# A hybrid convolution and recurrence block: HGRN's readout turned by VectorE and through memory, ahead of the convolution, and a layer norm with summed blocks

## The chip, the cores and the metric

The kernel runs on one core of a Trainium2 chip. The metric is the device time of one execution in microseconds (us), from the program's start to its end; a run lists it, and a profile of one execution gives a span that is a little shorter. A core has five engines that run their own instruction queues in order: TensorE (PE, matrix products, with its weight loads PEld), VectorE (DVE), ScalarE (ACT), GpSimd (POOL) and SyncE (SP). They wait for each other by semaphores. Transfers between memory and the core's on-chip memory are issued on such a queue and move on 16 DMA engines.

## The reference

One layer of a diffusion backbone, on 256 latent tokens of 2048 channels (and 256 context tokens that only prepare the states of the recurrence). All numbers are float32. What the change touches is the token mixer:

```
h = modulate(rms_norm(x, norm_pre_mix), sh_m, sc_m)
p_i, p_ff, p_fb, p_q, p_g, p_cv, p_cg, p_gc, p_gh = split_proj(h @ w_in)
o = hgrn_bidir(...)                    # 256 tokens x 8 heads x 128
# hgrn_readout
o = rms_norm(o, norm_g)                # mean of squares over the 128 channels of a head
y_h = (o * silu(p_g)) @ hgrn_out_w     # 1024 -> 2048
# conformer_branch
u = axial_dwconv(val * sigmoid(gate))  # 1024 channels: 512 along rows (31 taps), 512 along columns
u = silu(layer_norm(u, ln_g, ln_b))    # mean and variance over the 1024 channels
y_c = u @ conv_pw_w                    # 1024 -> 2048
y = (sigmoid(p_gc) * y_conv + sigmoid(p_gh) * y_hgrn) @ w_out
```

Behind it come a gated residual and a squared-ReLU MLP of 8192 channels.

## The kernel before

**Weights.** Each weight is read from memory as tiles of 128x1024 (`raw`, 512 KB), by transfers that SP issues into a ring of five buffers. For precision each tile is split: ScalarE writes a rounded high part `whi` (L124), and VectorE the remainder `wlo = raw - whi` (L127), into rings of four such pairs. The activations are split alike (`split`, L240), so a product is three products: high by high, high by low, low by high (`mm3r`). In `tokens` the tokens lie on the partitions of the result: one k step of 128 channels is 12 products of 512 columns (L188) for one pair `whi`, `wlo`. A projection of 2048 by 2048 has two groups of 16 k steps; the last three k steps of a group are done bank by bank, so that the evacuation of one bank lies beside the products of the next. Into the stream of weights further tiles are mixed that VectorE alone takes (matrix-vector products of the modulation, L1314 and L1301).

**Background work.** Everything else that has to happen beside the products is written as Python generators in a deque `bg`. After each k step `pump(us)` gives credit; the first three generators of the deque are advanced in turn. A generator that yields a number is charged that many us; one that yields `None` ends its turn for this k step, so some `None`s in a row let as many k steps go by. The instructions are written into the engines' queues at that place, each behind the weights' splits that were written last, and stay in that order. `finish` drains one generator.

**Order around the change.** Projection of the convolution's gates and values; then the generator `conv` is pushed (L829) and silu of HGRN's gate `p_g` is computed (`ev_g`, L831 to L839). Behind it the two readouts are pushed (L840, L841), four heads each, so in the deque they stand behind the convolution. Then come the two merge gates' projections (`ev_gate(0)`, `ev_gate(1)`, L853 and L854), 64 k steps in all, through which the background work is pumped. Then the product with `hgrn_out_w` (`ev_ho`), for which the readouts have to be finished, then the one with `conv_pw_w` (`ev_pw`), for which the convolution has to be finished, and the output projection and the MLP.

**`readout(j)`** (L1551) makes the reciprocal norms of four heads, scales the head's result `o` by it and by silu(g) on VectorE (L1562, two instructions of 128 columns per head, tokens on the partitions), then turns both halves on TensorE (L1567) into a bank, so that channels lie on the partitions; ScalarE takes the bank times the gain into the high part (L1570), VectorE the rest into the low part (L1571). The parts lie in `rp`, the operand of the heads' product.

**`conv`** (L1574) does 31 taps for four blocks of 128 channels on VectorE (L1584, L1586: 128x256 each, four to a charge of 1.6), then four blocks along the columns (L1592, L1595), and then the layer norm over 1024 channels, which lie as eight blocks of 256 columns in the two pages `y`. `sums` reduces each page's four blocks on VectorE (L1603) into one half of `lnred`; `mean` multiplies both halves by a 128x128 matrix that holds 1/1024 (`self.mean`), with two products that add up in one bank (L1609). That is done twice, for the mean and for the squares, and the normed result goes through silu into `cv`, the operand of the convolution's product.

**Turning without TensorE.** The MLP of the kernel before already turns its hidden result another way: VectorE turns blocks of 32x32 (`turn_blocks`, L1250), a page goes out to memory in one transfer and comes back in four that put the blocks in place (`swapped`, L1284 and L1287, issued by GpSimd). `turn_hidden` lets ten `None`s go by before it reads the page that comes back.

Of the kernel before, what the change touches and what calls it, by code (L numbers as in the profile page):

```python
# [8 lines left out]
F32 = mybir.dt.float32  # L9
# [3 lines left out]
AF = mybir.ActivationFunctionType  # L13
ALU = mybir.AluOpType

P = 128
T = 256
# [9 lines left out]
TW = 1024  # L27
# [7 lines left out]
PB = 4  # L35
# [102 lines left out]
class Kernel:  # L138
# [247 lines left out]
    def run(self):  # L386
        nc, a = self.nc, self.a
# [142 lines left out]
        for i in range(2):  # L530
            ps = self.bank()
# [172 lines left out]
        for k in range(KT):  # L704
            ps = self.bank()[:, :T]
            nk = KT if k < WHOLE else KP
            for t in range(nk // 4):
                st.fetch_to(FETCH)
                w = st.whole()
                for j in range(4):  # L710
                    g, n = 32 * j, 4 * t + j
# [68 lines left out]
        heads = []  # L780
        for h in range(NH):
            accs = []
            for d in range(2 * (h > 0)):
                accs.append(self.bank())
                for hf in range(2):
                    hi, lo = st.next()
# [50 lines left out]
            nc.vector.tensor_tensor(s, acc, s, op=ALU.mult)  # L837

        self.tokens(hlat, ev_g, 1.3, groups=1)  # L839
        for j in range(2):  # L840
            heads.append(self.push(self.readout(j)))  # L841


        gp = [[None] * 4, [None] * 4]
# [17 lines left out]

        self.tokens(self.operand(self.rp), ev_ho, 1.3, nk=8)
        self.finish(conv)
        zh, zl = self.pages(4, F32R, "zh"), self.pages(4, F32R, "zl")

# [684 lines left out]
    def readout(self, j):  # L1551

        nc = self.nc
        while self.ended < 4 * (j + 1):
            yield None
        r = self.osq[:, 8 * j:8 * j + 8]
        self.rstd(r, r, 1.0 / P)
        for h in range(4 * j, 4 * j + 4):
            o = self.at(self.on, h)
            for tb in range(2):  # L1560
                s = o[:, tb * P:(tb + 1) * P]
                nc.vector.scalar_tensor_tensor(s, s, self.osq[:, 2 * h + tb:2 * h + tb + 1], self.sg[tb][:, h * P:(h + 1) * P], op0=ALU.mult, op1=ALU.mult)  # L1562
            yield 0.5
            yield None
            ps = self.bank()
            for tb in range(2):
                nc.tensor.transpose(out=ps[:, tb * P:(tb + 1) * P], in_=o[:, tb * P:(tb + 1) * P], identity=self.v["ident"])  # L1567
            g = self.v["hng"][:, h:h + 1]
            hi, lo = self.rp[h][:, :T], self.rp[h][:, T:]
            nc.scalar.activation(out=hi, in_=ps[:, :T], func=AF.Copy, scale=g)  # L1570
            nc.vector.scalar_tensor_tensor(lo, ps[:, :T], g, hi.bitcast(F32), op0=ALU.mult, op1=ALU.subtract)  # L1571
            yield 0.5

    def conv(self, uhv, uvv):  # L1574
        nc, v = self.nc, self.v
        y = self.pages(2, F32, "conv")
        dww = v["dww"].rearrange("p (b w) -> p b w", b=8)
        out = lambda b: self.at(y, b).rearrange("p (r w) -> p r w", r=ROWS)
        n = 0
        for w in (PAD, *(w for w in range(CW) if w != PAD)):  # L1580
            for b in range(4):
                src, c = uhv[b][:, :, w:w + GW], dww[:, b, w:w + 1]
# [7 lines left out]
        for b in range(4, 8):  # L1590
            o, u = out(b), uvv[:, b - 4, :].rearrange("p (r w) -> p r w", r=ROWS)
# [5 lines left out]
        bc = lambda r: r.rearrange("p (o t) -> p o t", o=1).broadcast_to([P, PB, T])  # L1597
        kt_ = lambda pg: pg[:, :TW].rearrange("p (b t) -> p b t", b=PB)

        def sums(src):  # L1600
            red = self.small(512, "lnred")
            for j in range(2):
                nc.vector.tensor_reduce(red[:, j * T:(j + 1) * T], kt_(src[j]).rearrange("p b t -> p t b"), axis=mybir.AxisListType.X, op=ALU.add)  # L1603
            return red

        def mean(red):
            m = self.bank()
            for j in range(2):
                nc.tensor.matmul(m[:, :T], self.mean, red[:, j * T:(j + 1) * T], start=(j == 0), stop=(j == 1))  # L1609
            return m  # L1610
        red = sums(y)
        yield 2.4
        yield None
        yield None
        m = mean(red)
        yield None
        mu = self.small(T, "lnmu")
# [1 line left out]
        for j in range(2):  # L1619
            nc.vector.tensor_tensor(kt_(y[j]), kt_(y[j]), bc(mu), op=ALU.subtract)  # L1620
        yield 2.2
        sq = self.pages(2, F32, "lnsq")
        for j in range(2):
            nc.scalar.activation(out=sq[j][:, :TW], in_=y[j][:, :TW], func=AF.Square)
        yield None
        red = sums(sq)
        yield 2.4
        yield None
        yield None
        m = mean(red)  # L1630
        yield None
        self.rstd(m[:, :T], mu, 1.0)
# [4 lines left out]
        for b in range(0, 8, 2):  # L1637
            o, e = self.at(y, b, 2), self.at(sq, b, 2)
            for j in range(2):
                i, s = b + j, slice(j * T, (j + 1) * T)  # L1640
# [86 lines left out]
```

## Time and profile before

| | us |
|---|---|
| three runs: lowest, median, highest | 1624.18, 1625.0, 1625.57 |
| the profiled execution, its own time | 1623.7 |
| its span | 1621.9 |
| mean granted TensorE clock over the span | 0.999 |

The span is the time from the first to the last instruction that the profile records; 1.8 us of the execution lie around it. A row of the timeline gives a start, a duration, the engine, the line, the operation with its output and inputs, the shape, and in brackets an idle time ahead of it with what ended it; "x4" stands for that many alike in a row. A row of the windows gives a stretch, its length, and the busy time of each engine in it. A row of the groups gives the least, the median and the longest duration in ns, and when the group ran. The rows themselves stand in the prediction, beside what is read from them.

### The profile page before, as it was taken

The page shows a single profiled execution, that of the slowest core. Times are in us where ns is not written, and L with a number is a line of the kernel's source. Part 1 is how long each engine was busy: PE and PEld are TensorE (multiplying, and loading weights), DVE is VectorE, ACT ScalarE, POOL GpSimd, SP SyncE. Part 2 cuts the span into 40 slices and gives each one's busy share as a digit, 9 for nine tenths or more (in the row PEclk, how much of TensorE's full clock was granted, in tenths as well). Part 3 has the DMA queues.
Part 4 walks back from the last instruction along what each step waited for, and adds up shares of the span by engine and source line. Part 5 has one row for each costly group of instructions (what it writes and reads, how often), then busy time and mean ns, then how long its engine had stood idle before and what let it go on. Part 6 is the DMA issues. An engine that isn't in the chain of part 4 may idle for free.

```text
span 1621.9 us, 22046 instructions
## 1 busy us (share of the span) xinstructions
PE 1606.9 (99%) x8195; PEld 1322.7 (82%) x8195; DVE 1154.8 (71%) x1678; ACT 804.7 (50%) x1166; POOL 52.2 (3%) x98
## 2 busy tenths in 40 slices
PE   7999999999999999999999999999999999999998
PEld 5768888888888888888888888888888888888887
DVE  5886887787868889967887765555665665655556
ACT  6553454455654444653446665444443454435543
POOL 0000000000000000000000001000110011001000
PEclk9999999999999999999999999999999999999999
DMA  9997954444666556678887378866887688677773
GB/s 378 409 388 269 326 192 140 156 146 141 221 206 212 189 192 205 231 271 299 324 289 266 135 255 263 271 205 224 288 277 246 213 270 270 228 242 239 232 219 116
DMA packets 109148, 391.00 MB, mean 241 GB/s; under 512 B 12912, under 2 KB 13808, under 8 KB 109040
## 3 DMA queue, kind: packets, MB, share of 16 engines
q1 hardware_dynamic: 102096, 368.34, 66.3%
q0 software_dynamic: 6656, 20.99, 4.4%
q8 instruction: 64, 1.05, 0.3%
q14 instruction: 44, 0.36, 0.1%
q10 hardware_dynamic: 288, 0.26, 0.0%
HBM read 379.06 MB, written 10.49 MB: 240 GB/s over the span
## 4 chain that ended last, share of the span: by engine, by line
PE 92%; DMA 5%; DVE 1%; issue 1%; ACT 1%; SPq 0%; ACTq 0%; DVEq 0%
PE bank L188 80%; PE bank L255 5%; PE bank L257 3%; DMA raw<-wi 2%; DMA rawpage<-wm 1%; PE bank L1495 1%; DMA rawpage<-wms 1%; DMA x<-ctx 1%; PE bank L1541 0%; PE bank L1539 0%; PE bank L1530 0%; DVE wlo L127 0%; DMA raw<-wpw 0%; PE bank L1502 0%; ACT whi L124 0%
## 5 line engine op out<-in xcount | busy, mean ns | idle before, releaser
L127 DVE TENSOR_TENSOR wlo<-raw,whi 128x1024 fp32r<-128x1024 f32 x488 | 593.5, 1223 | 335.1 <-ACT whi L124 329.2
L124 ACT ACTIVATE whi<-raw 128x1024 fp32r<-128x1024 f32 x488 | 512.7, 1059 | 592.0 <-PE bank L188 388.2
L188 PE MATMUL bank<-whi,h 128*128 128x512 f32 x2160 | 674.1, 390 | 2.0 <-DVE h L673 1.1
L188 PEld LDWEIGHTS bank<-whi,h 128*128 128x128 f32 x2160 | 405.2, 188 | 87.4 <-DVE h L673 2.0
L188 PE MATMUL bank<-wlo,h 128*128 128x512 f32 x1080 | 420.9, 390 | 1.1 <-DVE wlo L127 1.1
L188 PEld LDWEIGHTS bank<-wlo,h 128*128 128x128 f32 x1080 | 202.8, 188 | 44.7 <-DVE wlo L127 3.0
L188 PE MATMUL bank<-whi,hidh 128*128 128x512 f32 x503 | 195.0, 388 | 0.0
L188 PE MATMUL bank<-wlo,hidh 128*128 128x512 f32 x503 | 195.0, 388 | 0.0
L188 PE MATMUL bank<-whi,hidl 128*128 128x512 f32 x503 | 195.0, 388 | 0.0
L188 PE MATMUL bank<-h,whi 128*128 128x512 f32 x512 | 164.7, 402 | 0.1
L188 PEld LDWEIGHTS bank<-h,whi 128*128 128x128 f32 x512 | 91.8, 188 | 23.4 <-issue 5.8
L188 PEld LDWEIGHTS bank<-wlo,hidh 128*128 128x128 f32 x503 | 94.5, 188 | 19.5
L188 PEld LDWEIGHTS bank<-whi,hidl 128*128 128x128 f32 x503 | 94.5, 188 | 19.3
L188 PEld LDWEIGHTS bank<-whi,hidh 128*128 128x128 f32 x503 | 94.5, 188 | 19.2
L188 PE MATMUL bank<-h,wlo 128*128 128x512 f32 x256 | 100.2, 391 | 0.0
L255 PE MATMUL bank<-h,whi 128*128 128x512 f32 x384 | 97.2, 395 | 0.0
L255 PEld LDWEIGHTS bank<-h,whi 128*128 128x128 f32 x384 | 69.0, 189 | 12.6
L1314 DVE SCALAR_TENSOR_TENSOR raw<-raw,silu_row 128x1024 f32<-128x1024 f32 x64 | 76.8, 1220 | 1.6 <-DMA raw<-wmt 1.5
L1301 DVE SCALAR_TENSOR_TENSOR gacc<-raw,silu_c,gacc 128x1024 f32<-128x1024 f32 x60 | 76.7, 1279 | 0.3 <-DMA raw<-wm 0.3
L188 PEld LDWEIGHTS bank<-h,wlo 128*128 128x128 f32 x256 | 48.0, 188 | 10.1
L257 PEld LDWEIGHTS bank<-h,wlo 128*128 128x128 f32 x384 | 52.4, 190 | 3.8
L257 PE MATMUL bank<-h,wlo 128*128 128x256 f32 x384 | 53.5, 282 | 0.0
(251 smaller groups left out, 1355.0 us busy)
## 6 DMA issues: line engine op xcount, KB each, us to landing
raw<-w SPq DMA_DIRECT2D x256, 512.0 KB, 4.7
raw<-wi SPq DMA_DIRECT2D x172, 512.0 KB, 4.3
raw<-wmt SPq DMA_DIRECT2D x64, 512.0 KB, 4.1
raw<-wm SPq DMA_DIRECT2D x64, 512.0 KB, 4.7
rawpage<-wm SPq DMA_DIRECT2D x42, 512.0 KB, 10.1
raw<-wo SPq DMA_DIRECT2D x32, 512.0 KB, 4.6
raw<-who SPq DMA_DIRECT2D x16, 512.0 KB, 4.9
raw<-wpw SPq DMA_DIRECT2D x16, 512.0 KB, 5.7
```

Source lines behind the costliest of these rows:

```text
L124: kn.his.append(nc.scalar.activation(out=hi, in_=raw, func=AF.Copy))
L127: kn.los.append(nc.vector.tensor_tensor(lo, raw, hi.bitcast(F32), op=ALU.subtract))
L188: ins = fn(*args, **kw)
L255: nc.tensor.matmul(bank, w[0][:, cut(i)], x(k)[2], start=(k == 0), stop=False)
L257: nc.tensor.matmul(bank[:, T:], w[1][:, cut(i)], x(k)[0], start=False, stop=(k == nk - 1))
L1301: nc.vector.scalar_tensor_tensor(acc, raw, s, acc, op0=ALU.mult, op1=ALU.add)
L1314: nc.vector.scalar_tensor_tensor(raw, raw, 1.0, self.srow, op0=ALU.mult, op1=ALU.mult, accum_out=self.dot[:, 32 * j + b:32 * j + b + 1])
L1495: nc.tensor.matmul(ps[64 * g:64 * g + 64, n * P + b * 64:n * P + b * 64 + 64], left[:, o:o + 64], right[:, r:r + 64] if right is not None ...
```

## The change

Three things. The readouts are put at the head of the deque, so their work is written ahead of the convolution's taps (`appendleft` of 1 and then 0, so readout 0 comes first). A readout scales its four heads, turns them with two block turns into a page `oflip` (L1251), sends this out and back by `swapped` (L1285, L1288), lets eight `None`s go by, and then for each head ScalarE takes the piece of `back` times the gain into `gained` (L1577), which is split into high and low like any activation (L240). And the norm's `sums` adds the eight blocks with three additions, of 1024, 512 and 256 columns, into one `lnred` of 256 columns, so that `mean` is one product. The page for the squares is taken earlier, as it holds the sums in between.

```diff
@@ -837,8 +837,9 @@
         self.tokens(hlat, ev_g, 1.3, groups=1)
-        for j in range(2):
-            heads.append(self.push(self.readout(j)))
+        for j in (1, 0):
+            heads.append(self.readout(j))
+            self.bg.appendleft(heads[-1])
@@ -1560,15 +1561,21 @@
                 nc.vector.scalar_tensor_tensor(s, s, self.osq[:, 2 * h + tb:2 * h + tb + 1], self.sg[tb][:, h * P:(h + 1) * P], op0=ALU.mult, op1=ALU.mult)
-            yield 0.5
+            if h % 2:
+                yield 0.5
+        flip = self.page(F32, "oflip")
+        for n in range(2):
+            self.turn_blocks(flip, n, self.on[j][:, n * 512:(n + 1) * 512])
+            yield 0.7
+        back = self.swapped(flip).rearrange("p (i b r) -> p b i r", i=4, b=8)
+        for _ in range(8):
             yield None
-            ps = self.bank()
-            for tb in range(2):
-                nc.tensor.transpose(out=ps[:, tb * P:(tb + 1) * P], in_=o[:, tb * P:(tb + 1) * P], identity=self.v["ident"])
-            g = self.v["hng"][:, h:h + 1]
-            hi, lo = self.rp[h][:, :T], self.rp[h][:, T:]
-            nc.scalar.activation(out=hi, in_=ps[:, :T], func=AF.Copy, scale=g)
-            nc.vector.scalar_tensor_tensor(lo, ps[:, :T], g, hi.bitcast(F32), op0=ALU.mult, op1=ALU.subtract)
+        for n in range(PB):
+            h = PB * j + n
+            g, src = self.v["hng"][:, h:h + 1], back[:, 2 * n:2 * n + 2]
+            t = self.small(T, "gained")
+            nc.scalar.activation(out=t.rearrange("p (b i r) -> p b i r", b=2, i=4), in_=src, func=AF.Copy, scale=g)
+            self.split(t, self.rp[h][:, :T], self.rp[h][:, T:])
             yield 0.5
@@ -1597,18 +1604,19 @@
-        def sums(src):
-            red = self.small(512, "lnred")
-            for j in range(2):
-                nc.vector.tensor_reduce(red[:, j * T:(j + 1) * T], kt_(src[j]).rearrange("p b t -> p t b"), axis=mybir.AxisListType.X, op=ALU.add)
+        def sums(src, both):
+            nc.vector.tensor_tensor(both[:, :TW], src[0][:, :TW], src[1][:, :TW], op=ALU.add)
+            nc.vector.tensor_tensor(both[:, :512], both[:, :512], both[:, 512:TW], op=ALU.add)
+            red = self.small(T, "lnred")
+            nc.vector.tensor_tensor(red, both[:, :T], both[:, T:512], op=ALU.add)
             return red
         def mean(red):
             m = self.bank()
-            for j in range(2):
-                nc.tensor.matmul(m[:, :T], self.mean, red[:, j * T:(j + 1) * T], start=(j == 0), stop=(j == 1))
+            nc.tensor.matmul(m[:, :T], self.mean, red, start=True, stop=True)
             return m
-        red = sums(y)
+        sq = self.pages(2, F32, "lnsq")
+        red = sums(y, sq[0])
@@ -1619,11 +1627,10 @@
-        sq = self.pages(2, F32, "lnsq")
-        red = sums(sq)
+        red = sums(sq, sq[0])
```

Line numbers of the kernel after are one higher than before from L841 on and seven higher inside `conv`. The rows below are instructions in the order of an engine's queue; "x2" are that many alike, and a number behind a name tells tiles of one name apart.

VectorE, early in the first merge gate's projection, where the queues first part. `conv_5035` is the page of the first four blocks, `uh_…` their inputs, `pack` the taps' weights, `osq` the reciprocal norms. Before:

```order
L1586 SCALAR_TENSOR_TENSOR conv_5035<-uh_4549,pack,conv_5035 128x256 x2
L1586 SCALAR_TENSOR_TENSOR conv_5035<-uh_4550,pack,conv_5035 128x256 x2
L127 TENSOR_TENSOR wlo<-raw,whi 128x1024 x2
L1586 SCALAR_TENSOR_TENSOR conv_5035<-uh_4549,pack,conv_5035 128x256 x2
L1586 SCALAR_TENSOR_TENSOR conv_5035<-uh_4550,pack,conv_5035 128x256 x2
L127 TENSOR_TENSOR wlo<-raw,whi 128x1024
```

And after, the end of the first readout's work and the second's:

```order
L1563 SCALAR_TENSOR_TENSOR o<-o,osq,silu_g_5012 128x128
L1251 STREAM_TRANSPOSE oflip<-o 128x4x4x32 x2
L384 RECIPROCAL osq<-osq 128x8
L127 TENSOR_TENSOR wlo<-raw,whi 128x1024
...
L127 TENSOR_TENSOR wlo<-raw,whi 128x1024
L1251 STREAM_TRANSPOSE oflip<-o 128x4x4x32 x2
L1593 SCALAR_TENSOR_TENSOR conv_5035<-uh_4549,pack,conv_5035 128x256 x2
L1593 SCALAR_TENSOR_TENSOR conv_5035<-uh_4550,pack,conv_5035 128x256 x2
L127 TENSOR_TENSOR wlo<-raw,whi 128x1024 x2
```

The left-out rows are the second readout's eight scalings (L1563). The taps stand behind both readouts now, and each later tap four batches further back against the weights.

ScalarE, from the last silu of HGRN's gate on; `gate` is the first merge gate's evacuation at the end of its first group. Before:

```order
L836 ACTIVATE silu_g_5012<-bank 128x512
L124 ACTIVATE whi<-raw 128x1024 x14
L850 ACTIVATE gate<-bank 128x512 x3
L124 ACTIVATE whi<-raw 128x1024 x2
L850 ACTIVATE gate<-bank 128x512
```

And after; the `h_…` are the parts of `rp`:

```order
L836 ACTIVATE silu_g_5012<-bank 128x512
L124 ACTIVATE whi<-raw 128x1024 x9
L1577 ACTIVATE gained<-back,pack 128x256 x2
L240 ACTIVATE h_370<-gained 128x256
L240 ACTIVATE h_458<-gained 128x256
L1577 ACTIVATE gained<-back,pack 128x256
L124 ACTIVATE whi<-raw 128x1024
L240 ACTIVATE h_549<-gained 128x256
```

The gain on `back` stands behind the ninth weight after the silu, with further weights of the same group queued behind it. On GpSimd the two readouts' transfers (one `there`, four `back` each) stand ahead of the loads of the output's gain rows, with nothing between them.

TensorE, in the second merge gate's projection, where the first mean stood; `h_…` is the activations' operand of a k step. Before:

```order
L188 MATMUL bank<-wlo,h_685 128x512
L188 MATMUL bank<-whi,h_685 128x512
L1609 MATMUL bank<-lnred,mean 128x256 x2
L1567 MATMUL bank<-pack,o 128x128 x2
L188 MATMUL bank<-whi,h_750 128x512
L188 MATMUL bank<-wlo,h_750 128x512
```

And after, where the first mean stands now:

```order
L188 MATMUL bank<-wlo,h_1089 128x512
L188 MATMUL bank<-whi,h_1089 128x512
L1616 MATMUL bank<-lnred,mean 128x256
L188 MATMUL bank<-whi,h_1152 128x512
L188 MATMUL bank<-wlo,h_1152 128x512
```

The first mean stands 84 of the gate's products behind the place where the first four transposes stood before (in the same projection, between `h_612` and `h_685`), and the second mean another 84 behind it. The sixteen transposes are gone from TensorE's queue.

## The prediction

> **What bounds the kernel now.** I read the page first: its busy line, then the chain that ended last.
>
> ```profile
> PE 1606.9 (99%) x8195; PEld 1322.7 (82%) x8195; DVE 1154.8 (71%) x1678; ACT 804.7 (50%) x1166; POOL 52.2 (3%) x98
> ...
> PE 92%; DMA 5%; DVE 1%; issue 1%; ACT 1%; SPq 0%; ACTq 0%; DVEq 0%
> ```
>
> TensorE (PE) is busy 99% of the span and carries 92% of the chain; VectorE (DVE) is next with 71%. So only what shortens TensorE's own queue, or makes it wait, can move the end. Then I read the stretches that the change touches: the rest of the first gate's projection, where the moved work arrives (545 to 640), the place it leaves (640 to 710), and the two products behind (710 to 800).
>
> ```profile
> 545.00:640.00 95.00, 95.00 (x420) 78.68 (x420) 81.24 (x145) 43.01 (x47) 0.00 (x0) 1.00 0.58 190
> 640.00:710.00 70.00, 69.81 (x313) 56.89 (x312) 63.91 (x87) 43.92 (x62) 1.20 (x2) 1.00 0.76 253
> 710.00:800.00 90.00, 89.83 (x397) 73.89 (x396) 67.16 (x66) 36.62 (x38) 2.13 (x4) 1.00 0.82 290
> ```
>
> The columns are PE, PEld, DVE, ACT, POOL busy, the granted clock, the DMA share. TensorE has next to no gap anywhere, at a granted clock of 1.00. VectorE has 14 us free of 95 in the first stretch and 6 of 70 in the second. So the sum is one of TensorE's time from start to start, and the danger is a VectorE or ScalarE queue that reaches TensorE late. TensorE's timeline gives the rest:
>
> ```profile
> 640.25 0.39 PE L188 MATMUL bank<-wlo,h 128*128 128x512 f32 x1
> ...
> 647.73 0.39 PE L188 MATMUL bank<-wlo,h 128*128 128x512 f32 x1
> 647.96 0.39 PE L188 MATMUL bank<-whi,h 128*128 128x512 f32 x1
> 648.53 1.12 PE L1567 MATMUL bank<-pack,o 128*128 128x128 f32 x4 [0.18 <-DVE o L1562]
> ...
> 649.72 0.40 PE L188 MATMUL bank<-wlo,h 128*128 128x512 f32 x1
> ...
> 652.00 0.39 PE L188 MATMUL bank<-whi,h 128*128 128x512 f32 x1
> 652.23 1.02 PE L1609 MATMUL bank<-lnred,mean 128*128 128x256 f32 x4
> 653.09 0.38 PE L1567 MATMUL bank<-pack,o 128*128 128x128 f32 x2
> ...
> 653.54 0.39 PE L188 MATMUL bank<-wlo,h 128*128 128x512 f32 x1
> ...
> 669.93 0.39 PE L188 MATMUL bank<-whi,h 128*128 128x512 f32 x1
> ...
> 671.47 0.39 PE L188 MATMUL bank<-wlo,h 128*128 128x512 f32 x1
> ...
> 677.62 0.39 PE L188 MATMUL bank<-wlo,h 128*128 128x512 f32 x1
> ...
> 680.57 0.40 PE L188 MATMUL bank<-wlo,h 128*128 128x512 f32 x1
> ...
> 695.77 0.39 PE L188 MATMUL bank<-whi,h 128*128 128x512 f32 x1
> 696.01 0.38 PE L1567 MATMUL bank<-pack,o 128*128 128x128 f32 x2
> 696.14 0.48 PE L188 MATMUL bank<-whi,h 128*128 128x512 f32 x1
> 696.46 0.39 PE L188 MATMUL bank<-wlo,h 128*128 128x512 f32 x1
> ...
> L1567 PE MATMUL bank<-pack,o x16: 270/273/330, 648.5 to 701.8; 128*128 128x128 f32 x16
> ```
>
> From 640.25 to 647.73 there are 33 products of 512 columns: 7.48 / 33 = **0.227 us each**, so one k step of 12 takes 2.72. The durations (390 ns) are longer only because products overlap. The reader is to measure each foreign group as the time from the high product ahead of it to the low product behind it, less two paces (0.453).
>
> **The change part by part.** Seven places leave or shrink.
> - 695.77 to 696.46 is 0.69: two transposes cost 0.24. Their starts are 0.13 apart (696.01 to 696.14), so 0.10 of it is the turn from one kind of product to the other and back. Four places are of this kind (also near 664, 667 and 701.5): 4 x 0.24 = 0.95.
> - 652.00 to 653.54 and 669.93 to 671.47 are 1.54 each: 1.09 over, with a mean's two products and two transposes; together 2.17. The products' own part is 652.23 to 653.09, 0.86, so 0.43 each.
> - 647.96 to 649.72 is 1.76: 1.31 over, for four transposes and a wait on L1562.
>
> Sum: 0.95 + 2.17 + 1.31 = **4.43 us** of TensorE's time now. What comes back is two single products: 2 x (0.43 + 0.10) = 1.06. One more trifle: from 677.62 to 680.57 twelve products take 2.95 in place of 2.72, in an order that has low products held back behind late VectorE work; the rows of the change have the plain order there. I take 0.2 as gained, bounds 0 and 0.23.
>
> TensorE: Matmul & The Clock Gate of the Trainium skill, Part 4: PE-mode transpose, puts a 128x128 transpose at about 275 ns in a kernel's context. L1567's row, 273 ns, agrees as a duration; but by that figure sixteen would take 4.4 us where the starts give 8 x 0.24 = 1.9, and the time would be 2.5 lower, 1619.4. The starts decide: two transposes have begun and given way within 0.13, so the sum stays.
>
> Next, what the new work can hold up. First VectorE, whose rows are these:
>
> ```profile
> 554.65 2.36 DVE L127 TENSOR_TENSOR wlo<-raw,whi 128x1024 fp32r<-128x1024 f32 x2
> ...
> 556.92 1.68 DVE L1586 SCALAR_TENSOR_TENSOR conv<-uh,pack,conv 128x256 f32<-128x256 f32 x4
> 558.51 1.23 DVE L127 TENSOR_TENSOR wlo<-raw,whi 128x1024 fp32r<-128x1024 f32 x1
> 559.64 1.68 DVE L1586 SCALAR_TENSOR_TENSOR conv<-uh,pack,conv 128x256 f32<-128x256 f32 x4
> ...
> 618.87 0.42 DVE L1592 TENSOR_SCALAR conv<-uv,pack 128x256 f32<-128x256 f32 x1
> ...
> 632.33 1.22 DVE L1314 SCALAR_TENSOR_TENSOR raw<-raw,silu_row 128x1024 f32<-128x1024 f32 x1
> ...
> 633.48 0.28 DVE L1595 SCALAR_TENSOR_TENSOR conv<-uv,pack,conv 128x64 f32<-128x64 f32 x1
> ...
> 648.12 1.14 DVE L1562 SCALAR_TENSOR_TENSOR o<-o,osq,silu_g 128x128 f32<-128x128 f32 x4
> 649.17 1.22 DVE L127 TENSOR_TENSOR wlo<-raw,whi 128x1024 fp32r<-128x1024 f32 x1
> ...
> L1250 DVE STREAM_TRANSPOSE turned<-rsq x32: 704/711/712, 958.1 to 1530.0; 128x512 f32<-128x512 f32 x32
> ```
>
> By starts: four convolution taps 1.59, one low half (wlo) 1.13, one L1314 1.15, one L1562 0.26; one block turn 0.71 (say 0.63 to the next start). The two readouts bring 16 x 0.26 + 4 x 0.63 + 2 x 0.13 = 6.9 us to the stretch from 557 on. In exchange the taps slide back: six batches of four, not ten, stand before the group's end, 6.4 us less. So the low halves reach the end of the first gate's first group 0.5 us later than now. The longest distance between two low halves is 1.13 + 8 x 0.26 + 2 x 0.63 + 0.13 = 4.6 us. A weight's pair is wanted three steps, 8.2 us, after its buffer was released, so this is hidden; a loss here I take as nothing (bounds 0, and the slower rival's price below). The block sums stand in place of the reduces, and L1571 goes; all of that lies behind 640.
>
> The second place is the first mean. In TensorE's queue of the change it stands 84 products behind the place of the first transposes, which a plain pace reaches at 647.96 + 0.23 = 648.19: so at 648.19 + 84 x 0.2267 = 667.2. Will the sum be there? The convolution ends later, so I add up VectorE's queue from the pair of weights that ScalarE (ACT) starts at 636.14:
>
> ```profile
> 572.22 1.06 ACT L124 ACTIVATE whi<-raw 128x1024 fp32r<-128x1024 f32 x1 [1.66 <-PE bank L188]
> ...
> 636.14 2.01 ACT L124 ACTIVATE whi<-raw 128x1024 fp32r<-128x1024 f32 x2
> ...
> 689.25 0.73 ACT L240 ACTIVATE h<-conv 128x256 fp32r<-128x256 f32 x2
> ```
>
> ScalarE's high half is there 0.97 later, at 637.1, and from then VectorE has no gap: 12 low halves 13.6, two tap batches 3.2, three L1314 3.45, the four vertical blocks (618.87 to 633.76, less five low halves and one L1314) 8.1, the sums of 1024, 512 and 256 columns (estimated as a low half, a half and a third of it) 2.1, small ones 0.2. That is 30.6, so 667.7: **TensorE waits 0.5 us**. Bounds: 0, since 0.5 is 2% of the 30.6, and 1.6, one low half's time more, if one raw tile is late. The second mean comes 84 products later and its sum some 9 us before it.
>
> The third is ScalarE's queue. Behind its ninth weight after the silu (572.22, done 573.3) stands the gain on `back`, which waits for two transfers in a row on GpSimd (POOL):
>
> ```profile
> L1284 POOL DMA_DIRECT2D there<-turned x16: 538/561/566, 960.3 to 1531.0; - x16
> ...
> DMA to landing us min/median/max: 2.9/6.1/9.8
> L1287 POOL DMA_DIRECT2D back<-there x64: 552/552/574, 964.8 to 1542.2; - x64
> ...
> DMA to landing us min/median/max: 3.8/6.6/9.0
> ```
>
> The first readout's blocks are turned by 554.65 + 2.27 + 0.13 + 1.13 + 2.1 + 1.26 = 561.5. With 0.3 to issue, a median 6.1, three issues of 0.55 and 6.6 the last piece lands at 576.2; ScalarE waits 2.9. Behind that stand five gains and splits (0.36 each, as in the row of 689.25) and the next weight's high half, done at 579.0. VectorE comes to its low half at 561.5 + 5.7 (the second readout and two low halves) + 10.9 (four tap batches, four low halves) = 578.1, and has then two low halves, two batches and two more low halves to the group's last, 585.8. That one is wanted by the eighth product after 572.22 + 5 x 2.72 = 585.8, at 587.4. So 1.6 is spare and 0.9 is used: nothing lost, but with little left. The DMA share here is 0.58, the lowest of the three stretches. The second readout's wait falls before a weight of the next group, wanted 8.2 us later. Sixteen small ScalarE operations in place of eight lie in its 52 idle us. The convolution ends some 10 us later and is first read behind the heads' product, which alone takes 16 x 2.72 = 43.5.
>
> **Sum:** -4.43 - 0.2 + 1.06 + 0.5 = -3.1 us. Against the profiled execution, 1623.7 (span 1621.9 and 1.8 around it), that is 1620.6; that execution lies 1.3 below the median, 1625.0, and the forecast is for the median: **1621.9 us**.
>
> **The rivals.**
> - *No wait at the mean:* VectorE is a little quicker, and the full 3.6 is gained: 1621.4. For it: 0.5 us on a sum of 30 is 2%.
> - *A longer wait at the mean:* VectorE 1.1 further behind, as one late raw tile before an L1314 would put it: 2.0 gained, 1623.0. For it: nothing in its queue is idle from 637 on, so any delay there arrives whole.
> - *TensorE gains it and loses it again:* the products behind 710 take weights with a DMA share of 0.82; were they bound by it, nothing would be left: 1624.5. Against it: TensorE's gap there is 0.17 of 90.
> - *Slower, transfers late:* at both maxima the piece lands at 561.8 + 9.8 + 1.65 + 9.0 = 582.3. The next high half is then done at 585.1, its low half at 586.2, and behind it VectorE has two tap batches and three low halves to the group's last: 586.2 + 3.2 + 3.4 = 592.8, wanted at 587.4. TensorE stands 5.4, the mean's wait is swallowed, and 5.4 - 3.6 = 1.8 is lost: 1626.8. It costs one for one from a landing at 576.9 on, and turns the sign at 580.5. Against it: both maxima at once.
>
> SBUF — State Buffer of the Trainium skill, Who interferes with whom, holds that a VectorE instruction with two SBUF inputs contends with a GpSimd instruction that reads SBUF. By that rule GpSimd's issues beside a full VectorE come late, and the time is this last rival's, 1626.8. The trace bears it out little: GpSimd's issues of pieces all take 552 to 574 ns.
>
> That the change does not do what it says is no rival: TensorE's rows of the change hold none of the transposes.
>
> **How the numbers follow.** Forecast 0.55; no wait 0.13; longer wait 0.14; lost again 0.08; transfers late 0.10. About 0.2%, 3.25 us, is what a measurement of this kernel tells from no change, and my forecast lies right under it: half of its chance and all of "no wait" count as faster, 0.40; the other half, the longer wait and "lost again" as the same, 0.50; late transfers 0.10. The range runs from 1620.9 (the whole gain and 0.5 of run-to-run spread) to 1625.2 and leaves out the late transfers and the edges.
>
> **What would show it.** Right: no transposes on TensorE between 640 and 706; single means about 0.53 over the pace each; a wait on the block sum at the first, near 667; none in 545 to 640. Wrong: an idle time on TensorE near 587 put down to low halves; ScalarE waiting for `back` over 4 us; or gaps behind 710 that the trace of before lacks.

## The result and the profile after

Over 22 runs of each kernel the kernel after takes 1622.64 us in the median (1621.4 to 1624.57), the one before 1624.88 (1623.5 to 1625.8). That is 2.24 us less, a ratio of 0.9987 with a 95% interval of 0.9982 to 0.9993. The forecast was 1621.9 in the median, 3.1 less. The profiled execution of the kernel after took 1624.24 us, 1.6 above that median, with a span of 1622.5, 0.6 more than that of before; only one of the 22 runs took longer (1624.57).

First the page of the kernel after (busy times, then the chain that ended last), and the same three stretches (length, then PE, PEld, DVE, ACT, POOL busy, granted clock, DMA share, GB/s).

```profile
PE 1605.2 (99%) x8175; PEld 1321.6 (81%) x8175; DVE 1152.7 (71%) x1684; ACT 807.2 (50%) x1174; POOL 57.6 (4%) x108
...
PE 92%; DVE 3%; DMA 2%; ACT 1%; issue 1%; SPq 0%; ACTq 0%; DVEq 0%
```

```profile
545.00:640.00 95.00, 95.00 (x421) 78.67 (x419) 79.34 (x139) 48.96 (x64) 5.59 (x10) 1.00 0.65 213
640.00:710.00 70.00, 69.90 (x309) 57.61 (x308) 63.23 (x97) 41.54 (x54) 1.10 (x2) 1.00 0.73 251
710.00:800.00 90.00, 88.17 (x385) 71.80 (x384) 68.68 (x69) 36.53 (x40) 2.16 (x4) 1.00 0.83 293
```

The first two stretches are as forecast: no gap where the work arrives, none where it left. The third is not: TensorE stands idle for 1.83 of 90 us, where it was 0.17 before. To see when time is gained and lost, take the evacuations of the banks, which follow TensorE, and count from the last one of silu(g), ahead of the change. ScalarE's and VectorE's timeline, before:

```profile
551.01 0.58 ACT L836 ACTIVATE silu_g<-bank 128x512 f32<-128x512 f32 x1
...
685.88 0.58 ACT L850 ACTIVATE gate<-bank 128x512 f32<-128x512 f32 x1
...
729.89 0.58 ACT L850 ACTIVATE gate<-bank 128x512 f32<-128x512 f32 x1
...
776.06 0.68 DVE L861 TENSOR_TENSOR gate<-bank,gate 128x512 f32<-128x512 f32 x1
...
956.86 0.58 ACT L1238 ACTIVATE relu<-bank 128x512 f32<-128x512 f32 x1
```

And after:

```profile
552.13 0.58 ACT L836 ACTIVATE silu_g<-bank 128x512 f32<-128x512 f32 x1
...
683.56 0.58 ACT L851 ACTIVATE gate<-bank 128x512 f32<-128x512 f32 x1
...
728.90 0.58 ACT L851 ACTIVATE gate<-bank 128x512 f32<-128x512 f32 x1
...
775.07 0.68 DVE L862 TENSOR_TENSOR gate<-bank,gate 128x512 f32<-128x512 f32 x1
...
957.39 0.58 ACT L1239 ACTIVATE relu<-bank 128x512 f32<-128x512 f32 x1
```

From the first row to the second it is 134.87 before and 131.43 after: 3.44 us gained by the middle of the second merge gate. At the end of that gate 2.11 are left, at the end of the heads' product 2.11, and at the MLP's first evacuation 0.59, which stays to the end. (That the first rows differ by 1.12 is the program's start, which the change does not touch.) So the forecast gain was there, and 2.85 us of it were given back between 690 and 957 in this execution. TensorE's timeline shows where:

```profile
719.70 0.94 PE L188 MATMUL bank<-whi,h 128*128 128x512 f32 x2
721.40 0.50 PE L188 MATMUL bank<-wlo,h 128*128 128x512 f32 x1 [0.76 <-DVE wlo L127]
...
785.72 0.61 PE L188 MATMUL bank<-whi,h 128*128 128x512 f32 x2
787.18 0.50 PE L188 MATMUL bank<-wlo,h 128*128 128x512 f32 x1 [0.85 <-DVE wlo L127]
...
788.32 0.50 PE L188 MATMUL bank<-wlo,h 128*128 128x512 f32 x1 [0.17 <-DVE wlo L127]
```

Two products from 719.70 to 721.40 take 1.70 in place of 0.45, and two from 785.72 take 1.46. Both times a low half is late. The chain of the kernel after says what was late behind it (start, length, what):

```profile
712.90 6.02 DMA raw<-wi
719.02 1.07 ACT whi L124
720.12 1.24 DVE wlo L127
721.40 49.08 PE bank L188 x215
...
774.05 6.60 DMA raw<-wpw
780.75 1.06 ACT whi L124
```

A weight's load took 6.0 and 6.6 us. The experiments ask why.

### The profile page after: what moved, and what is told of

Same layout as the page of the kernel before. It is cut to its first block, busy times and chain, and to the rows that moved or that the text cites. A ratio compares the mean times of both kernels' runs of the same rounds, so it can differ in the third digit from the quotient of the medians.

```text
span 1622.5 us, 22041 instructions
## 1 busy us (share of the span) xinstructions
PE 1605.2 (99%) x8175; PEld 1321.6 (81%) x8175; DVE 1152.7 (71%) x1684; ACT 807.2 (50%) x1174; POOL 57.6 (4%) x108
## 3 DMA queue, kind: packets, MB, share of 16 engines
q8 instruction: 64, 1.05, 0.3%
## 4 chain that ended last, share of the span: by engine, by line
PE 92%; DVE 3%; DMA 2%; ACT 1%; issue 1%; SPq 0%; ACTq 0%; DVEq 0%
PE bank L188 80%; PE bank L255 5%; PE bank L257 3%; DVE wlo L127 1%; PE bank L1496 1%; DMA raw<-wpw 1%; DMA raw<-wi 1%; DMA x<-ctx 1%; ACT whi L124 1%; PE bank L1542 0%; PE bank L1540 0%; PE bank L1531 0%; DVE conv L1602 0%; DVE gacc L1302 0%; PE bank L1503 0%
```

## The experiments

All times are medians of 11 runs, beside 33 of the kernel before on the same chip; the first row alone has the 22 runs of each from the result. The columns of gains are worked out as above, from the profiled execution of each kernel against that of before; minus is earlier.

| kernel | at 686 | at 730 | at 776 | end | median | before | ratio, 95% interval |
|---|---|---|---|---|---|---|---|
| after, first trace | -3.44 | -2.11 | -2.11 | -0.59 | 1622.64 | 1624.88 | 0.9987, 0.9982 to 0.9993 |
| again | -3.43 | -3.27 | -3.27 | -1.19 | 1623.55 | 1624.53 | 0.9992, 0.9983 to 1.0000 |
| norm_only | -1.80 | -1.92 | -1.92 | -1.70 | 1622.35 | 1624.53 | 0.9987, 0.9978 to 0.9996 |
| te_ahead | -1.78 | -1.87 | -1.87 | -1.96 | 1623.12 | 1624.53 | 0.9992, 0.9983 to 1.0000 |
| tail_late | -3.44 | -3.52 | -3.05 | -1.49 | 1622.91 | 1624.53 | 0.9989, 0.9980 to 0.9998 |
| te_dummy | -1.78 | -1.87 | -1.87 | -1.90 | 1622.73 | 1624.57 | 0.9987, 0.9978 to 0.9996 |
| te_pages | -1.86 | -1.95 | -1.95 | -2.01 | 1623.37 | 1624.57 | 0.9992, 0.9983 to 1.0001 |
| xr_late | -3.44 | -3.29 | -3.29 | -3.85 | 1621.18 | 1624.57 | 0.9981, 0.9972 to 0.9990 |
| wm_less | -3.44 | -3.53 | -3.53 | -0.96 | 1624.98 | 1624.57 | 1.0002, 0.9994 to 1.0011 |
| fetch_back | -3.42 | -3.51 | -3.51 | -3.57 | 1621.42 | 1624.38 | 0.9981, 0.9972 to 0.9989 |
| te_fetch | -1.78 | -1.87 | -1.87 | -1.96 | 1623.42 | 1624.38 | 0.9993, 0.9984 to 1.0002 |
| before_xr | -0.05 | -0.04 | -0.04 | -0.58 | 1623.42 | 1624.38 | 0.9997, 0.9989 to 1.0006 |
| late_back | +1.66 | +1.56 | +1.57 | +2.72 | 1628.37 | 1624.38 | 1.0025, 1.0016 to 1.0034 |

The intervals of the eleven runs are about 0.09% to each side, 1.5 us, so the medians tell only the large steps apart. The traces tell the rest, but each is one execution of its kernel.

**again: the kernel after once more.** No edit.

> The kernel after, once more, for a second trace. Theory 1 (late tail): the last part of the convolution's norm now runs some 18 us later, 694 to 711, and keeps ScalarE and VectorE from the weights just ahead of the second merge gate's last three steps, so a weight's load goes out late and TensorE waits. It expects a wait on a low half near 721 again, 1.0 to 1.7 us, and a time of 1622.6 +- 0.7. Theory 2 (transfers): that wait was chance in one execution, and it is the convolution product's weights near 786 and 812 that give back what is gained, because the transfers are full there; it expects under 0.4 us of wait near 721 and over 1 us near 786.

The wait near 721 was not there (0.16 between 686 and 730), and 2.08 were lost behind 776. So the 721 wait was not a fixed cost of the late norm tail. Theory 1 is weak already; theory 2 has the place.

**norm_only: the new sums and single means on the kernel before.**

```diff
-            red = self.small(512, "lnred")
-            for j in range(2):
-                nc.vector.tensor_reduce(red[:, j * T:(j + 1) * T], kt_(src[j]).rearrange("p b t -> p t b"), axis=mybir.AxisListType.X, op=ALU.add)
+            nc.vector.tensor_tensor(both[:, :TW], src[0][:, :TW], src[1][:, :TW], op=ALU.add)
...
-            for j in range(2):
-                nc.tensor.matmul(m[:, :T], self.mean, red[:, j * T:(j + 1) * T], start=(j == 0), stop=(j == 1))
+            nc.tensor.matmul(m[:, :T], self.mean, red, start=True, stop=True)
```

> The kernel before with the new sums and one product per mean alone. Both: each of the two places with a mean shrinks from 1.09 to about 0.66 over the pace (0.43 less, one product of two), 0.86 together. Theory 1: no new wait near 721, and the 0.86 stays to the end: 1624.0. Theory 2: the 0.86 is lost again by 815: 1624.9, ratio 1.000.

TensorE's timeline of this kernel, at the first four transposes and at the first mean:

```profile
649.55 0.39 PE L188 MATMUL bank<-whi,h 128*128 128x512 f32 x1
649.78 0.60 PE L1567 MATMUL bank<-pack,o 128*128 128x128 f32 x4
...
650.45 0.40 PE L188 MATMUL bank<-wlo,h 128*128 128x512 f32 x1
...
652.76 0.39 PE L188 MATMUL bank<-whi,h 128*128 128x512 f32 x1
652.99 0.59 PE L1609 MATMUL bank<-lnred,mean 128*128 128x256 f32 x2
...
653.88 0.39 PE L188 MATMUL bank<-wlo,h 128*128 128x512 f32 x1
```

The mean with its pair of transposes is 1.12 less 0.45, 0.67 over the pace, as expected (1.09 before). But the four transposes are only 0.90 less 0.45, 0.45 over, where they were 1.31 before: 0.86 of that place was a wait for VectorE, and cheaper sums on VectorE remove it without touching a transpose: the scalings (L1562) that the transposes wait for begin at 647.96 here and at 648.12 before, which is 1.76 earlier when counted from silu(g). So the norm alone gains 1.80 of the 3.44, twice the 0.86 that was expected, and keeps 1.70 of it to the end.

**te_ahead: the kernel after with TensorE's turns, queued ahead.**

```diff
+            ps = self.bank()
+            for tb in range(2):
+                nc.tensor.transpose(out=ps[:, tb * P:(tb + 1) * P], in_=o[:, tb * P:(tb + 1) * P], identity=self.v["ident"])
...
-        back = self.swapped(flip).rearrange("p (i b r) -> p b i r", i=4, b=8)
```

> The kernel after with the old readout (turned by TensorE), but queued ahead of the convolution, so the norm's tail stands at the same weights as in the kernel after. Theory 1: eight pairs of transposes at 0.24 come back, 1.9 us, between 560 and 590, and the wait near 721 stays, so 1622.6 + 1.9 = 1624.5, about the kernel before. Theory 2: what the transposes cost was lost behind 780 anyway, so about 1622.8.

The sixteen transposes cost 2.03 at the first gate's first evacuation (590.10 less 551.22, against 587.86 less 551.01), 0.127 each. The norm's tail stands where it does in the kernel after, and there is no wait at 721; nothing is lost behind 776 either. Both theories fall short: what is lost belongs neither to the late tail nor to that place as such.

**tail_late: the norm's tail beside the heads' product.**

```diff
         self.rstd(m[:, :T], mu, 1.0)
         yield 1.7
+        for _ in range(14):
+            yield None
```

> The kernel after with fourteen k steps let go by between the norm's reciprocal root and its last part, which then runs beside the heads' product (from about 735) and no longer ahead of the second gate's end. Theory 1: the wait near 721 is gone, and with it 1.3 us: 1621.3; if VectorE's 7 us more in the heads' product make a wait of their own there, up to 1 of it is lost. Theory 2: no wait to remove, 1622.6.

No wait at 721, 0.47 lost beside the heads' product, and again 1.56 behind 776. Moving the tail does not help.

What sets the kernels apart now: the three traces with block turns lost 1.5 to 2.1 behind 776, where the first two weights landed 6.4 to 6.8 us after their issue; the kernels with TensorE's turns lost 0.2 or nothing, at 5.4 to 5.6.

**te_dummy and te_pages: do GpSimd's transfers or the ring of pages do it?** Both are te_ahead, with this behind each readout, te_dummy:

```diff
+        self.page(F32, "oflip")
+        self.swapped(self.on[j])
```

and te_pages:

```diff
+        for _ in range(2):
+            nc.scalar.copy(out=self.page(F32, "unused")[:, :1], in_=self.v["ident"][:, :1])
```

> Offsets are against the kernel before, counted from the last evacuation of silu(g) near 551. The kernel queued ahead with TensorE's turns (te_ahead), which kept its 1.9 us to the end, plus two unused round trips of the readout's page through memory by GpSimd, with the same four more pages as the kernel after. Theory 3: the round trips or the pages change how the x loads and the convolution product's weights land at 772 (6.3 to 6.8 us after issue in the three kernels with block turns, 5.4 to 5.6 in the others), so 1.5 us is lost between 776 and 816, and the end stands at -0.4. Theory 4: they have no part in it, only how early TensorE comes; then the landing is 5.5 and the end stands at -1.9.

> The same kernel with four more pages that stay unused (one column written by ScalarE), and no transfers. If the shift of the ring of pages is what makes the landings longer: 6.5 us at 772 and an end at -0.4. If the GpSimd transfers are: 5.5 and an end at -1.9, as in te_ahead.

Neither loses anything. Theory 3 falls.

**xr_late: the x loads out of the way.** These are four loads of x for the residual, 2 MB, which GpSimd issues from 772 to 795 in the kernel after; here they are held until the output projection.

```diff
-            if g == 0 and 7 < k < 12:
-                j = k - 8
+            if g == 0 and k in (5, 7, 9, 11):
+                j = k // 2 - 2
+                with self.tc.issue_after(self.his[-1].ins):
+                    nc.scalar.copy(out=xr[j][:, :1], in_=self.v["ident"][:, :1])
```

> The kernel after, with the four loads of x for the residual (2 MB, now issued between 772 and 796) held by a one-column write of ScalarE until the output projection's weights 217 to 222, near 825 to 845. If the transfers are what gives the gain back: the first two weights behind 772 land in under 5.2 us, the waits near 786 and 812 go, and the end stands at -3.2 (1621.3 in the median). If they are not, it stays as in the kernel after: -0.6 to -1.2. If 2 MB more beside the output projection make waits of their own, those show between 825 and 860.

The timeline of SP and ScalarE in this kernel:

```profile
771.93 1.52 SPq L86 DMA_DIRECT2D raw<-wpw  x2
...
776.58 1.06 ACT L124 ACTIVATE whi<-raw 128x1024 fp32r<-128x1024 f32 x1 [4.03 <-DMA raw<-wpw]
```

The weight is split 4.65 us after its issue, TensorE has no wait left between 730 and 900, and the whole gain reaches the end, with 0.56 more, which the kernel before loses there itself. Its median, 1621.18, is the lowest of all.

**wm_less: four modulation tiles moved behind.**

```diff
-                gemv(b % 2)
+                gemv(b % (4 if nm == "wpw" else 2) == 1)
```

> The kernel after, with four of the eight modulation tiles beside the convolution's product moved behind, into the output projection (2 MB of loads and 4 x 1.2 us of VectorE out of 770 to 815). Transfers or VectorE behind the weights in that stretch are the cause: waits near 786 and 812 go, the end stands at -3.2. Being early is the cause in itself: no change, -0.6 to -1.2.

Nothing is lost up to 838 (-4.08 there). Then the modulation itself is late, and TensorE waits for the residual:

```profile
905.76 0.39 PE L188 MATMUL bank<-whi,zl 128*128 128x512 f32 x1
908.89 0.66 PE L188 MATMUL bank<-pack,y 128*128 128x128 f32 x4 [2.74 <-DVE y L965]
```

So taking these tiles out of that stretch is enough as well, but they have no room behind it. They also take four instructions of about 1.2 us off VectorE there, so this run alone does not tell transfers from VectorE.

**fetch_back and te_fetch: TensorE's own instructions.** Two queues of the page are of kind "instruction". One has 64 packets of 16 KB in every kernel here (the other moves 0.36 MB and is left aside):

```profile
q8 instruction: 64, 1.05, 0.3%
```

TensorE's 8,195 products and as many weight loads are 16,390 instructions, 64 bytes each if these 1.05 MB are theirs: one packet for 256 instructions, 128 products, 29 us at the pace of 0.227. In the kernel before, the packets from 711 on begin 29.4, 29.9, 29.8 and 25.5 us apart. That the queue is TensorE's is inferred from this. For each trace the table has the fifth of a us in which the packet begins, against the issue of the first two weights behind 771:

| kernel | weights issued | packet begins | after the issue | split begins | issue to split |
|---|---|---|---|---|---|
| before | 773.84 | 770.6 | -3.2 | 779.41 | 5.57 |
| norm_only | 773.52 | 770.8 | -2.7 | 779.02 | 5.50 |
| te_ahead | 772.18 | 769.4 | -2.8 | 777.62 | 5.44 |
| te_dummy | 772.19 | 767.4 | -4.8 | 777.77 | 5.58 |
| te_pages | 771.97 | 767.8 | -4.2 | 777.48 | 5.51 |
| after | 772.85 | 776.2 | +3.3 | 779.48 | 6.63 |
| again | 771.76 | 774.8 | +3.0 | 778.11 | 6.35 |
| tail_late | 771.15 | 774.6 | +3.5 | 777.95 | 6.80 |

In all eight, an x load was issued 0.7 us ahead of the two weights, and a modulation tile 2.3 and two further weights 4.1 us behind them, so the issues around them do not differ. The change takes 16 transposes and one product of each of the two means out of TensorE's queue, 20 in the page's count (8,195 less 8,175), so every later packet is wanted at another place of the program. The edits: fetch_back is the kernel after with sixteen unused products at the program's start, and te_fetch is te_ahead without the sixteen warming products near 18 us.

```diff
+        self.warm(16)
         srow = self.page(F32, "srow")[:, :TW]
```

```diff
-            self.warm(16)
```

> Theory 3 has fallen (te_dummy and te_pages ended at -1.9 and -2.0). Theory 5: TensorE's instructions come in transfers of 16 KB, one for each 128 products, each about 0.95 us of one DMA engine. The change takes 16 transposes out ahead of 770, so the fetch that fell 2 to 5 us ahead of the first two weights behind 772 now falls while they are in transit, and they land 1 us later (after, again, tail_late), and the next fetch does the same near 803. This kernel is the one after with 16 unused products at the very start, where TensorE waits for its first data anyway; the fetches are back at the places of te_ahead. Expected: first landing 5.3 to 5.7, under 0.5 lost between 776 and 816, end at -3.0, median near 1621.3. If the fetch has no part: 6.3 to 6.8, 1.5 to 2 lost, end at -0.6 to -1.5.

> The other way round: te_ahead, which lost nothing, with the 16 warming products ahead of 20 us left out, so the fetch moves 16 products later, into the transit of the weights behind 772. Theory 5: first landing 6.3 to 6.8, about 1.2 lost between 776 and 816, end at -0.7 (counted from 551, so without what the missing warming does at the start). If the fetch has no part: 5.5, nothing lost, -1.9.

fetch_back does what theory 5 says. SP's and ScalarE's timeline, and the queues from the issue to the split (packets, MB, share of 16 engines), first of the kernel after:

```profile
772.85 1.52 SPq L86 DMA_DIRECT2D raw<-wpw  x2
...
779.48 1.06 ACT L124 ACTIVATE whi<-raw 128x1024 fp32r<-128x1024 f32 x1 [6.01 <-DMA raw<-wpw]
```

```profile
q1 hardware_dynamic: 378, 1.42, 54.9%
q0 software_dynamic: 144, 0.52, 29.1%
q8 instruction: 1, 0.02, 0.9%
```

Then of fetch_back:

```profile
771.20 1.52 SPq L86 DMA_DIRECT2D raw<-wpw  x2
...
776.74 1.06 ACT L124 ACTIVATE whi<-raw 128x1024 fp32r<-128x1024 f32 x1 [4.93 <-DMA raw<-wpw]
```

```profile
q1 hardware_dynamic: 258, 0.96, 47.0%
q0 software_dynamic: 144, 0.52, 36.5%
```

The packet's 0.9% of 16 engines over 6.63 us is 0.95 us of one engine. With it in transit the weight is 1.09 us later (6.63 against 5.54); without it nothing is lost behind 776, and the median falls by 2.96 in place of 2.24 (22 runs) and 0.98 (again). Theory 4, that it is only how early TensorE comes, falls with it: fetch_back comes as early as the kernel after. The intervals of the ratios overlap, so the medians agree with theory 5 and do not prove it. The sixteen products also take one bank more at the start, which is not tested apart; up to 730 the trace is like those of wm_less and tail_late (-3.51 against -3.53 and -3.52). te_fetch did not test the other direction: its packet began at 770.6, still 2.0 ahead of the issue at 772.55, since the place of a packet varies by some us from run to run. Issue to split of 5.49 and no loss agree, but the other direction stays unshown.

Two kernels without the x loads in this stretch (before_xr follows below) add to the table:

| kernel | weights issued | packet begins | after the issue | split begins | issue to split |
|---|---|---|---|---|---|
| before_xr | 774.04 | 770.4 | -3.6 | 777.36 | 3.32 |
| xr_late | 771.93 | 772.8 | +0.9 | 776.58 | 4.65 |

So in xr_late, too, the packet was in transit with the weights, and the split came 1.3 us later than in before_xr (which also lacks the change); but at 4.65 the weight was still early enough. In these traces the large losses behind 776 are those with both, the x loads and the packet.

The loss has a second place. By the starts of TensorE's products, 0.46, 1.28 and 0.34 us more go between 808 and 819 in after, again and tail_late. The next packet began 1.2 to 1.9 behind the issue of two weights there (802.14, 801.30, 800.58), which were split 7.4 to 7.8 us after their issue; in fetch_back it began 0.4 ahead and they were split after 5.8. But in te_fetch it began 1.2 behind too, they were split after 6.8, and nothing was lost; before and te_ahead have 6.9 and 7.0 with the packet 1.6 ahead. So at this place the packet is likely a part and not shown as the cause.

At 721 the packet alone does not explain the wait. In the kernel after it began 1.8 us behind the issue of the weight at 712.90, the weight was split 6.1 us after its issue, and 1.33 were lost. In fetch_back, te_ahead, te_dummy and te_pages it began ahead of that weight's issue, the split came after 4.5 to 4.8, and nothing was lost. But in again, xr_late and wm_less it began 0.7 to 1.1 behind the issue, the split came after 4.9 to 5.2, and at most 0.16 was lost. What made the 6.1 of the one execution stays open.

**before_xr: the x loads moved on the kernel before.** The edit of xr_late.

> The kernel before with the x loads held as in xr_late. Its own wait near 787 (0.45 over the pace) goes, so an end at -0.45. Then the change, with the x loads out of the way in both kernels, is worth 3.85 - 0.45 = 3.4, all that its steps on TensorE give. If the x loads cost the kernel before more than its visible wait, up to -1.

-0.58 in the trace, no difference that the medians can tell. With the x loads out of the way in both, the change is worth 3.85 - 0.58 = 3.27 in the traces and 1623.42 (beside 1624.38) against 1621.18 (beside 1624.57), 2.4 in the medians.

**late_back: the transfers late.**

```diff
         nc.gpsimd.dma_start(there, page[:, :TW])
+        if again:
+            first, there = there, self.dr.tile([P, TW], F32, name="there2", tag="there2", bufs=2)
+            nc.gpsimd.dma_start(there, first)
...
-        back = self.swapped(flip).rearrange("p (i b r) -> p b i r", i=4, b=8)
+        back = self.swapped(flip, True).rearrange("p (i b r) -> p b i r", i=4, b=8)
```

> The slower rival made real: the kernel after with one more copy in memory between the way out and the way back, so the pieces land some 6 us later, 581 to 583 (the gain on ScalarE stands one weight further back by the same program). By the prediction's rule, one us for each that they land behind 576.9 plus one weight's 2.7, so 1.5 to 3.5 us of wait on TensorE near 587 or at the next weights, and an end near +0.5 to +2.5 against the kernel before. If ScalarE's queue has more spare than I gave it: no wait there, and an end as in the kernel after.

ScalarE's and TensorE's timeline, and the link of the chain ahead of it:

```profile
589.87 0.60 ACT L851 ACTIVATE gate<-bank 128x512 f32<-128x512 f32 x1 [1.44 <-PE bank L188]
595.32 0.91 ACT L1580 ACTIVATE gained<-back,pack 128x256 f32<-128x256 f32 x2 [4.85 <-DMA back<-there]
...
596.24 0.39 PE L188 MATMUL bank<-whi,h 128*128 128x512 f32 x1
598.72 0.50 PE L188 MATMUL bank<-whi,h 128*128 128x512 f32 x1 [2.08 <-ACT whi L124]
```

```profile
587.65 7.56 DMA back<-there
```

The first readout's pieces make ScalarE wait 2.94 us (until 578.92), which delays no product. It is the second readout, not the first, that stops TensorE by way of ScalarE: in this kernel's queue it stands between two evacuations of the gate, with the next group's weights behind it. At the group's last evacuation TensorE is 5.0 us late, and the kernel is slower than before, 1628.37 against 1624.38. The end of the trace, +2.72, lies a little above the 0.5 to 2.5 that were expected.

## Why the prediction was right, and where not

**TensorE's sum was right, a little too small.** Forecast -3.1 with a wait at the first mean; the traces have -3.44 at 686 and, where nothing is lost at 721, -3.27 to -3.53 at 730. (At 686 the second mean of the kernel after and two pairs of transposes of the one before are still to come, 0.44 against two times 0.24.) That the median came out only 0.7 above the forecast is partly luck: about 0.4 more was gained, and about 1.2 was lost. The single means are below the 0.53 that was forecast:

```profile
668.11 0.39 PE L188 MATMUL bank<-whi,h 128*128 128x512 f32 x1
668.60 0.70 PE L1616 MATMUL bank<-lnred,mean 128*128 128x256 f32 x2
...
669.36 0.39 PE L188 MATMUL bank<-wlo,h 128*128 128x512 f32 x1
...
687.97 0.39 PE L188 MATMUL bank<-whi,h 128*128 128x512 f32 x1
688.20 0.59 PE L1616 MATMUL bank<-lnred,mean 128*128 128x256 f32 x2
...
688.86 0.40 PE L188 MATMUL bank<-wlo,h 128*128 128x512 f32 x1
```

The second is 0.89 less 0.45, 0.44 over the pace. The first is 0.80, so 0.36 of it is the wait for the block sum (forecast 0.5); counted from the start of before, 1.12 earlier, the sum is there at 668.60 - 1.12 = 667.5, forecast 667.7.

**Transposes by starts, not durations.** te_ahead measures 0.127 us each; the forecast had 0.24 for two. TensorE: Matmul & The Clock Gate of the Trainium skill, Part 4: PE-mode transpose, gives about 275 ns, next to a figure for bf16, and these transposes are float32; as the length of one that agrees with the trace, as the price of one in a full queue it does not, and the time by it, 1619.4, was not reached.

**What goes with the transposes was split wrongly, without harm to the sum.** The 1.31 at the first four was put down to them and a wait on their scaling; norm_only shows that 0.86 of it leaves with the cheaper sums. Of the 3.44 at 686, the norm alone gives 1.80, which leaves 1.64 for the turning.

**ScalarE's wait for the pieces was there, and hidden.**

```profile
573.33 1.06 ACT L124 ACTIVATE whi<-raw 128x1024 fp32r<-128x1024 f32 x1 [1.66 <-PE bank L188]
575.00 0.91 ACT L1577 ACTIVATE gained<-back,pack 128x256 f32<-128x256 f32 x2 [0.60 <-DMA back<-there]
```

0.6 us where 2.9 were forecast (the kernel's start lies 1.1 later in this trace, and the pieces were read at 575.0, not 576.2), and no wait on TensorE between 545 and 640. GpSimd's issues were not late beside VectorE either: the four pieces took 2.18 us to issue in the kernel after, 0.55 each.

**The slower rival had the mechanism and the wrong readout.** late_back shows that a later return costs more than the whole gain. But the forecast priced the first readout and let the second one pass as wanted 8.2 us later; in late_back it is the second that lies between the gate's evacuations and delays TensorE, and the first cost nothing.

**The step that failed: nothing late behind 710.** Of "gained and lost again" the prediction said that the gap there is 0.17 of 90, so the loads do not bind, and gave it 0.08. The prediction's own sign of being wrong, gaps behind 710 that the trace of before lacks, came true (1.83 idle us against 0.17). The rival's place was right and its mechanism, a full DMA share, half of it. With 2 MB less beside them nothing is lost (xr_late), though the packet was in transit there as well, so the full transfers have a part; but with the same loads nothing is lost either when the instruction packet is elsewhere (fetch_back). In the three traces that lost most behind 776 the change had moved that packet into the transit of two weights. The prediction counted what the change takes off TensorE's time, and not that taking 18 products out also moves the fetches. In the median of 22 runs 1.2 of the 3.44 us are missing (3.44 - 2.24). So the mechanism of the gain was right, and the sum lacked a term for what is lost behind it. fetch_back shows the packet's part in the loss near 786; the wait near 721 (in one of the two traces of this kernel) and the packet's part near 812 stay open, and how often a run meets them was not measured.

## What to carry to other kernels

A gain on the busiest engine is only safe if the next loads have spare: look behind the place of the change for the first weights behind a group's end, and at what else is moving there; holding 2 MB that were not urgent kept the whole gain here (xr_late, 1621.18). When instructions are removed from a long queue, small losses can appear elsewhere that have nothing to do with the work removed, as the 1.5 to 2.1 us here, and the instruction queue's packets are one thing to look at before blaming what stands there. Do the halves of a change apart: the norm's half alone came to 1622.35, within the noise of the whole.

## What the runs showed of the hardware

An instruction packet of 16 KB took about 0.95 us of one DMA engine. With it in transit a 512 KB load was split 1.09 us later beside the x loads (6.63 against 5.54 us from issue to split, after and fetch_back), and 1.33 later without them (4.65 against 3.32, xr_late and before_xr). If the queue is TensorE's, as its 64 packets for 8,195 products suggest, one comes for each 128 products. Its place varies from run to run: counted from the last silu(g), the packet near 772 began 216 to 218 us later in te_ahead, te_dummy and te_pages, and 220 to 224 later in after, again, tail_late and xr_late. That may be part of why runs of the kernel after spread over 3.2 us; it was not tried.
